# A row softmax on one core: sixteen-row transfers, and the scaling of 13 of 16 groups on GpSimd

## The chip, the core and the metric

The kernel runs on one core of a Trainium2 chip. Four of the core's engines matter: VectorE (DVE in the profile), ScalarE (ACT), GpSimd (POOL) and SyncE (SP, which only issues transfers here). Transfers between the memory of the chip (HBM) and the on-chip memory run on the core's 16 DMA engines; SP and ACT each feed a queue of them. The metric is device time in microseconds (us), the median of several runs.

## What is computed

A softmax over the last axis of 16 x 1024 x 512 numbers in fp32, that is 16384 rows of 512:

```python
x_max = np.max(x, axis=-1, keepdims=True)
exp_x = np.exp(x - x_max)
return (exp_x / np.sum(exp_x, axis=-1, keepdims=True)).astype(np.float32)
```

The input is 33.55 MB, the output as much. There is no matrix product.

## The kernel before

The 16384 rows are laid on 128 partitions, 128 rows of 512 to each. They are cut into eleven chunks. A chunk of R rows per partition is one load, for which each partition reads R consecutive rows. The chunks have 1, 3, 5, 7 and then seven times 16 rows (`CHUNKS`, line 13; the second number of each pair is the place in the on-chip tile). The tile `held` has room for 96 of the 128 rows of a partition (line 79), so the last two chunks go where the first ones and chunk 5 lay: load 9 is issued after the store of chunk 3 and load 10 after the store of chunk 4 (`AFTER_STORE`, line 20), and each waits until the stores that free its place have landed. The other nine loads are issued at the start (lines 138 and 139). Two of them, chunk 0 on ACT and chunk 1 on SP, are moved ahead of the barrier at which all engines meet at the start (`AT_HEAD`, line 30, and `loads_at_the_head`).

Work goes by groups of up to 8 rows per partition, 18 in all (lines 83 to 91). For each group:

- `rowmax` (line 102): DVE reduces the group to the negated maximum of each row, tile `shift`;
- `exps` (line 110): ACT takes the exponential of each row in place, one instruction a row, with `shift` as its bias, and the sum of the row as a by-product, tile `sums`. In the trace each is an ACTIVATE and an ACTIVATION_READ_ACCUMULATOR;
- `scale` (lines 122 and 124): DVE takes the reciprocals of the sums, tile `recip`, and multiplies each row by its own, one instruction a row;
- the store (line 130), issued on ACT's queue. It stands in ACT's order of instructions, behind whatever exponentials were emitted before it. Chunks 4, 5 and 6 are stored in halves of 8 rows (`STORE_ROWS`, line 26), the others whole.

The order is written out by hand (lines 137 to 150) and each engine keeps to it: maximum and exponentials of group g, then the scaling of group g - 1. At the four first changes of chunk (`FINISH_BEFORE`, line 24) the scaling of the earlier group comes before the maximum of the new one. Waits between engines, and between transfers and engines, are put in by the framework from what each instruction reads and writes.

GpSimd has nothing to do but four small MEMSETs at the start.

Of the kernel before, what the change touches and what calls it, by code (L numbers as in the profile page):

```python
# [1 line left out]

# [4 lines left out]

F32 = mybir.dt.float32
EXP = mybir.ActivationFunctionType.Exp
AX = mybir.AxisListType.X  # L10


CHUNKS = [
    (1, 0), (3, 1), (5, 4), (7, 9), (16, 16), (16, 32), (16, 48), (16, 64), (16, 80),
    (16, 0), (16, 16),
]
SBUF_ROWS = 96

EARLY = 9
AFTER_STORE = {3: [9], 4: [10]}  # L20

GROUP = 8

FINISH_BEFORE = (1, 2, 3, 4)

STORE_ROWS = {4: 8, 5: 8, 6: 8}

ON_ACT = (0,)

AT_HEAD = {mybir.EngineType.Activation: 1, mybir.EngineType.SP: 1}  # L30

def loads_at_the_head(nc):

    main, body = nc.main_func.blocks[0], nc.main_func.blocks[1]
    for engine, count in AT_HEAD.items():
        loads = [
            i
            for i in body.instructions  # L40
            if i.engine == engine and type(i).__name__ == "InstDMACopy"
        ][:count]
        barrier = next(
            n
            for n, i in enumerate(main.instructions)
            if i.engine == engine and type(i).__name__ == "InstDrain"
        )
        for load in loads:
            body.instructions.remove(load)
        main.instructions[barrier:barrier] = loads  # L50


@with_exitstack
def kernel(
    ctx: ExitStack,
    tc: tile.TileContext,
    x: bass.AP,
    out: bass.AP,
):
    nc = tc.nc  # L60
    nc.at_finalize(loads_at_the_head)
    P = nc.NUM_PARTITIONS

    x_flat = x.flatten_outer_dims()
    out_flat = out.flatten_outer_dims()
    n, d = x_flat.shape
    assert n == P * sum(R for R, _ in CHUNKS)


    src, dst, at = [], [], 0  # L70
    for R, _ in CHUNKS:
        for flat, views in ((x_flat, src), (out_flat, dst)):
            part = flat[at : at + P * R, :]
            views.append(part.rearrange("(p r) d -> p r d", r=R))
        at += P * R

    data = ctx.enter_context(tc.tile_pool(name="data", bufs=1))
    stats = ctx.enter_context(tc.tile_pool(name="stats", bufs=4))
    held = data.tile([P, SBUF_ROWS, d], F32, name="held")
    place = [held[:, s : s + R, :] for R, s in CHUNKS]  # L80


    groups = []
    for k, (R, _) in enumerate(CHUNKS):
        m = max(1, round(R / GROUP))
        cuts = [R * i // m for i in range(m + 1)]
        since = 0
        for a, b in zip(cuts, cuts[1:]):
            ends = b == R or b - since >= STORE_ROWS.get(k, R)
            groups.append((k, a, b, since if ends else None))  # L90
            since = b if ends else since
    shift = [None] * len(groups)
    sums = [None] * len(groups)

    def load(k):
        queue = nc.scalar if k in ON_ACT else nc.sync
        queue.dma_start(out=place[k], in_=src[k])

    def rowmax(g):
        k, a, b, _ = groups[g]  # L100
        shift[g] = stats.tile([P, b - a], F32, name="shift", tag="shift")
        nc.vector.reduce_max(  # L102
            out=shift[g], in_=place[k][:, a:b, :], axis=AX, negate=True
        )

    def exps(g):
        k, a, b, _ = groups[g]
        sums[g] = stats.tile([P, b - a], F32, name="sums", tag="sums")
        for r in range(a, b):
            nc.scalar.activation(  # L110
                out=place[k][:, r, :],
                in_=place[k][:, r, :],
                func=EXP,
                bias=shift[g][:, r - a : r - a + 1],
                scale=1.0,
                accum_out=sums[g][:, r - a : r - a + 1],
            )

    def scale(g):
        k, a, b, since = groups[g]  # L120
        recip = stats.tile([P, b - a], F32, name="recip", tag="recip")
        nc.vector.reciprocal(out=recip, in_=sums[g])  # L122
        for r in range(a, b):
            nc.vector.tensor_scalar_mul(  # L124
                out=place[k][:, r, :],
                in0=place[k][:, r, :],
                scalar1=recip[:, r - a : r - a + 1],
            )
        if since is not None:
            nc.scalar.dma_start(  # L130
                out=dst[k][:, since:b, :], in_=place[k][:, since:b, :]
            )
        if b == CHUNKS[k][0]:
            for later in AFTER_STORE.get(k, ()):
                load(later)

    with tc.manual_schedule():
        for k in range(EARLY):
            load(k)
        waiting = None  # L140
        for g, (k, a, _, _) in enumerate(groups):
            if waiting is not None and a == 0 and k in FINISH_BEFORE:
                scale(waiting)
                waiting = None
            rowmax(g)
            exps(g)
            if waiting is not None:
                scale(waiting)
            waiting = g
        scale(waiting)  # L150


# [1 line left out]
_INS = ['x']  # L154
_OUTS = [((16, 1024, 512), 'float32')]


# [23 lines left out]
```

## Time and profile before

| | us |
|---|---|
| median of 3 runs | 161.63 (161.62 to 161.69) |
| profiled execution, first to last instruction (span) | 160.1 |
| DVE busy | 124.2 |
| ACT busy | 93.4 |
| POOL busy | 0.2 |
| first maximum starts | 4.9 |
| last store issued | 146.4 |

The span is that of one execution under the profiler; the runs are timed from outside and hold 1.5 us more. The busy times are sums over an engine's instructions; issuing a transfer is not in them. In the lines below a group of instructions is given as: line, engine, operation, tile written <- tiles read, shapes (partitions x elements), count | total busy us, mean ns of one | idle time of the engine before them and what ended it. A line of DMA issues has the count, the size of each and the median time from issue to landing, which holds the time in the queue. The rows of digits divide the span into 40 slices of 4.0 us, with the busy share in tenths.

### The profile page before, as it was taken

How to read it: one execution, taken by the hardware profiler on the slowest of the kernel's cores; microseconds unless marked ns; L12 is line 12 of the kernel's file. 1: busy time of each engine (PE TensorE's matmuls, PEld its weight loads, DVE VectorE, ACT ScalarE, POOL GpSimd, SP SyncE). 2: the span in 40 equal slices, each digit the busy share in tenths (PEclk: the TensorE clock that was granted, in tenths of full speed). 3: DMA queues.
4: the chain of work that ended last, by engine and by line, in shares of the span. 5: the costliest groups of instructions: out<-in, count | busy, mean ns of one | idle time of the engine just before them, and what ended most of it. 6: DMA issues, size and time to landing. Idle time of an engine off the chain costs nothing.

```text
span 160.1 us, 525 instructions
## 1 busy us (share of the span) xinstructions
DVE 124.2 (78%) x164; ACT 93.4 (58%) x257; POOL 0.2 (0%) x4
## 2 busy tenths in 40 slices
DVE  0349094299699999999999999999999999935000
ACT  0550805604994959595959595959586867760000
POOL 0000000000000000000000000000000000000000
DMA  7999979989899999998999999999999999999993
GB/s 237 411 400 475 490 320 465 459 359 489 377 435 465 401 471 442 418 426 385 446 479 430 397 456 401 458 393 446 413 458 483 409 409 442 450 409 418 483 409 156
DMA packets 3603, 67.14 MB, mean 419 GB/s; under 512 B 400, under 2 KB 400, under 8 KB 912
## 3 DMA queue, kind: packets, MB, share of 16 engines
q10 hardware_dynamic: 2160, 33.82, 49.3%
q1 hardware_dynamic: 1440, 33.29, 49.1%
q14 instruction: 3, 0.02, 0.0%
HBM read 33.55 MB, written 33.55 MB: 419 GB/s over the span
## 4 chain that ended last, share of the span: by engine, by line
DVE 71%; ACT 15%; DMA 3%; issue 2%; DVEq 0%; ACTq 0%
DVE shift L102 39%; DVE held L124 30%; ACT held L110 14%; DMA held<-in_x_dram 3%; DVE recip L122 2%; ACT L110 1%; DVEq L176 0%; ACTq L110 0%
## 5 line engine op out<-in xcount | busy, mean ns | idle before, releaser
L110 ACT ACTIVATE held<-held,shift 128x512 f32<-128x512 f32 x128 | 90.5, 708 | 44.5 <-DVE shift L102 32.3
L102 DVE TENSOR_REDUCE shift<-held 128x8 f32<-128x4096 f32 (+4 forms) x18 | 70.8, 3938 | 4.9 <-DMA held<-in_x_dram 4.9
L124 DVE TENSOR_SCALAR held<-held,recip 128x512 f32<-128x512 f32 x128 | 52.3, 481 | 0.6
L110 ACT ACTIVATION_READ_ACCUMULATOR held<-held,shift 128x1 f32 x128 | 23.8, 186 | 0.0
L122 DVE RECIPROCAL recip<-sums 128x8 f32<-128x8 f32 (+4 forms) x18 | 3.4, 191 | 16.6 <-ACT held L110 16.6
L110 ACT ACT_TABLE_LOAD x1 | 1.3, 1283 | 4.9 <-DMA held<-in_x_dram 4.9
L165 POOL MEMSET const-bfloat16-1.0<- 128x1 bf16 x1 | 0.1, 102 | 0.0
L165 POOL MEMSET const-uint8-127<- 128x1 uint8 x1 | 0.1, 102 | 0.0
L165 POOL MEMSET const-float32-1.0<- 128x1 f32 x1 | 0.1, 99 | 0.0
L165 POOL MEMSET const-float32-0.0<- 128x1 f32 x1 | 0.1, 98 | 0.2 <-issue 0.2
## 6 DMA issues: line engine op xcount, KB each, us to landing
held<-in_x_dram SPq DMA_DIRECT2D x7, 4096.0 KB, 32.0
out_dram<-held ACTq DMA_DIRECT2D x4, 4096.0 KB, 19.8
out_dram<-held ACTq DMA_DIRECT2D x6, 2048.0 KB, 35.9
held<-in_x_dram SPq DMA_DIRECT2D x1, 1792.0 KB, 12.1
out_dram<-held ACTq DMA_DIRECT2D x1, 1792.0 KB, 27.0
held<-in_x_dram SPq DMA_DIRECT2D x1, 1280.0 KB, 8.0
out_dram<-held ACTq DMA_DIRECT2D x1, 1280.0 KB, 24.2
held<-in_x_dram SPq DMA_DIRECT2D x1, 768.0 KB, 4.6
```

The costliest lines, as they stand in the source:

```text
L102: nc.vector.reduce_max(out=shift[g], in_=place[k][:, a:b, :], axis=AX, negate=True)
L110: nc.scalar.activation(out=place[k][:, r, :], in_=place[k][:, r, :], func=EXP, bias=shift[g][:, r - a : r - a + 1], scale=1.0, accum_out=s ...
L122: nc.vector.reciprocal(out=recip, in_=sums[g])
L124: nc.vector.tensor_scalar_mul(out=place[k][:, r, :], in0=place[k][:, r, :], scalar1=recip[:, r - a : r - a + 1],)
L165: nc = _bacc.Bacc("TRN2", target_bir_lowering=False, num_devices=1)
```

## The change

All eight chunks now have 16 rows, and every load and store is one whole chunk of 4096 KB. The tile still has six places of 16 rows; six loads are issued at the start, load 6 after store 0 and load 7 after store 1. Only SP's first load stands ahead of the barrier. There are 16 groups of 8 rows, numbered from 0. For groups 0 to 12 the multiplication by the reciprocals is one GpSimd instruction over the whole group, with the 8 reciprocals of a partition broadcast along the rows; groups 13, 14 and 15 are scaled on DVE, row by row, as before. The reciprocals stay on DVE. Stores stay on ACT's queue. For chunks 0 to 3 a store is emitted one group later than it could be (`STORE_BEHIND`). The rule of `FINISH_BEFORE` goes, and the pool of the small tiles has 6 buffers for each of them in place of 4.

```diff
-CHUNKS = [
-    (1, 0), (3, 1), (5, 4), (7, 9), (16, 16), (16, 32), (16, 48), (16, 64), (16, 80),
-    (16, 0), (16, 16),
-]
-SBUF_ROWS = 96
-EARLY = 9
-AFTER_STORE = {3: [9], 4: [10]}
+CHUNK = 16
+CHUNKS = 8
+PLACES = 6
 GROUP = 8
-FINISH_BEFORE = (1, 2, 3, 4)
-STORE_ROWS = {4: 8, 5: 8, 6: 8}
-ON_ACT = (0,)
-AT_HEAD = {mybir.EngineType.Activation: 1, mybir.EngineType.SP: 1}
+STORE_BEHIND = [1, 1, 1, 1, 0, 0, 0, 0]
+LOAD_AFTER = {0: 6, 1: 7}
+ON_POOL = 13
+AT_HEAD = {mybir.EngineType.SP: 1}
...
+    def load(k):
+        nc.sync.dma_start(out=place(k), in_=x_rows[k])
+
+    def store(k):
+        nc.scalar.dma_start(out=out_rows[k], in_=place(k))
+        if k in LOAD_AFTER:
+            load(LOAD_AFTER[k])
...
     def scale(g):
-        k, a, b, since = groups[g]
-        recip = stats.tile([P, b - a], F32, name="recip", tag="recip")
+        recip = stats.tile([P, GROUP], F32, name="recip", tag="recip")
         nc.vector.reciprocal(out=recip, in_=sums[g])
-        for r in range(a, b):
+        if g < ON_POOL:
+            nc.gpsimd.tensor_mul(
+                out=rows(g),
+                in0=rows(g),
+                in1=recip.unsqueeze(2).to_broadcast([P, GROUP, d]),
+            )
+            return
+        for r in range(GROUP):
             nc.vector.tensor_scalar_mul(
...
     with tc.manual_schedule():
-        for k in range(EARLY):
+        for k in range(PLACES):
             load(k)
-        waiting = None
-        for g, (k, a, _, _) in enumerate(groups):
-            if waiting is not None and a == 0 and k in FINISH_BEFORE:
-                scale(waiting)
-                waiting = None
+        stored = 0
+        for g in range(groups):
             rowmax(g)
             exps(g)
-            if waiting is not None:
-                scale(waiting)
-            waiting = g
-        scale(waiting)
+            if g:
+                scale(g - 1)
+            if stored < CHUNKS and g > (stored + 1) * per - 1 + STORE_BEHIND[stored]:
+                store(stored)
+                stored += 1
+        scale(groups - 1)
+        while stored < CHUNKS:
+            store(stored)
+            stored += 1
```

`per` is 2, the groups of a chunk. So in ACT's order store 0 stands behind exponentials 3, stores 1, 2 and 3 behind exponentials 5, 7 and 9, store 4 behind exponentials 10, store 5 behind 12, store 6 behind 14 and store 7 at the end.

## The prediction

> **What bounds the kernel now.** I read the page's shares first, then the slices of DMA, the DMA issues, the chain, and last the windows of ten microseconds.
>
> ```profile
> span 160.1 us, 525 instructions
> DVE 124.2 (78%) x164; ACT 93.4 (58%) x257; POOL 0.2 (0%) x4
> DMA  7999979989899999998999999999999999999993
> HBM read 33.55 MB, written 33.55 MB: 419 GB/s over the span
> DVE 71%; ACT 15%; DMA 3%; issue 2%; DVEq 0%; ACTq 0%
> out_dram<-held ACTq DMA_DIRECT2D x6, 2048.0 KB, 35.9
> ```
>
> The reader is to see two full resources. The chain names DVE with 71%, but the chain follows instructions, and the last of them is the issue of a store. The DMA row stands at 9 or just under from the second slice to the last but one, and the 2 MB stores take 35.9 us from issue to landing: they stand in a queue. The windows say the same of both:
>
> ```profile
> 60.00:70.00 10.00, 9.96 (x17) 8.03 (x23) 0.00 (x0) 1.00 0.99 426
> 70.00:80.00 10.00, 9.96 (x14) 8.01 (x23) 0.00 (x0) 1.00 0.98 421
> 80.00:90.00 10.00, 9.96 (x11) 6.75 (x20) 0.00 (x0) 1.00 1.00 429
> ```
>
> Columns: window, its length, busy DVE, ACT and POOL, clock, DMA share, GB/s. The ten windows from 40 to 140 us have a mean of 432 GB/s. 33.55 + 33.55 = 67.1 MB at 432 GB/s is 155.4 us, so of the span of 160.1 only 4.7 us are not full-rate transfer, most of it in the first slice (237 GB/s over 4.0 us, 1.8 us lost) and the last (156 GB/s, 2.6 us lost). So the kernel is bound by **DMA**, with DVE full beside it from 34 to 143 us. Relief for DVE alone buys nothing. The most that better transfers can buy is a part of 4.7 us.
>
> The measured median is 161.63 us, 1.5 us over the profiled span of 160.1 (the part outside the first and last instruction); I add 1.5 to every span.
>
> **The change, part by part.** The rows that price it:
>
> ```profile
> L110 ACT ACTIVATE held<-held,shift 128x512 f32<-128x512 f32 x128 | 90.5, 708 | 44.5 <-DVE shift L102 32.3 <-issue 12.1
> L102 DVE TENSOR_REDUCE shift<-held 128x8 f32<-128x4096 f32 x14 | 61.7, 4411 | 0.0
> L124 DVE TENSOR_SCALAR held<-held,recip 128x512 f32<-128x512 f32 x128 | 52.3, 481 | 0.6
> L165 POOL MEMSET const-float32-1.0<- 128x1 f32 x1 | 0.1, 99 | 0.0
> ```
>
> and from the chain in order of time (start, length, what), the steps of one group of 8 rows, out of the last two groups:
>
> ```profile
> 132.66 4.34 DVE shift L102
> ...
> 137.08 5.76 ACT held L110 x16
> 142.83 0.02 issue
> 142.86 0.21 DVE recip L122
> 143.07 0.03 issue
> 143.10 0.49 DVE held L124
> ```
>
> So a group costs 4.4 us for the maximum (DVE), 5.8 for the exponentials with their sums (ACT), 0.3 for the reciprocal with its handovers and 3.3 for the scaling (the chain shows the eight multiplications of a full group as one piece of 3.26 us).
>
> *Removed from DVE:* 13 groups x 3.26 = 42.4 us of scaling. By the first part it buys nothing by itself, as DMA is the bound.
>
> *Added on POOL:* 13 instructions of 128x4096, each with two operands, the tile and the broadcast reciprocals. No row shows POOL do arithmetic, so I call its time P and bound it. From below: the reduction reads the same 128x4096 once in 4.41 us, and P should not be less than one such pass. From above: a pass for each operand and one for the result, 3 x 4.41 + 0.10 (POOL's own MEMSET of one element) = 13.3 us. I take 2 x 4.41 + 0.10 = **8.92 us**: the row nearest to it is the reduction, whose time goes by the elements it reads, and this instruction has twice as many operand elements. 13 x 8.92 = 116.0 us. Both ends stay for the range.
>
> The Trainium skill bears on this row ("GPSIMD Engine Reference", section 3.1): it gives a two-input elementwise operation on GpSimd 4497 ns at 2048 fp32 elements against 2293 on VectorE, and advises VectorE for such work. That speaks against the change; doubled it would be an estimate of 8.99 us, and the sum below would be 0.9 us longer.
>
> *Who waits for POOL.* The groups of POOL follow one another: a group's exponentials cost ACT 5.8 us against 8.92, so POOL is never short of work after its first. A store is issued by ACT, in order with the exponentials, and waits there for both its POOL groups. Behind store k stand the exponentials of the next groups, so ACT falls into POOL's pace: the store of chunk 5 stands ahead of exponentials 13 (groups counted from 0) and waits for POOL group 11. The sum from the start:
>
> - First load, now 16 rows, 4.19 MB: lands at 11.5 us. At 432 GB/s it is 9.7 us; in the trace of before the first three slices (237, 411, 400 GB/s) have moved that much by 12.0 us in small pieces. I take 11.5; the ends move the sum by -1.8 and +0.5.
> - Maximum 0, exponentials 0, reciprocal 0: 4.4 + 5.8 + 0.3, so POOL starts at 22.0.
> - 13 groups on POOL: 22.0 + 116.0 = 138.0.
> - DVE scales group 13. Its reciprocal is there at 22.0 + 12P + 5.8 + 0.4, which is P - 6.2 = 2.7 us before POOL ends group 12. Whether it may run beside POOL the trace can't show; the wait costs 0 to 2.7 us. I take 2.7: DVE's scaling passes 512 elements in 3.26 / 8 = 0.41 us, the reduction in 4.33 / 8 = 0.54, so it draws on the memory harder than the reductions that run beside POOL. Scaling 13 ends at 141.3.
> - Behind it on DVE stands maximum 15 (it was put after scaling 13 by the loop): 145.7. Exponentials 15: 151.5. Reciprocal and scaling 15: 155.1.
> - Last store, 4.19 MB with nothing before it in the queue (store 6 was issued at 141.3 and is through by 153): 9.7 us plus the start and landing. The last store of before took 12.9 us from issue to landing, with some backlog in it; I take 11.6, landed at 166.7. The ends are -1.9 and +1.3.
> - The span of before ends 0.85 us after its last landing: 167.6. With 1.5: **169.1 us**.
>
> In short T = 53.1 + 13P, and 160 to 162 needs P between 8.2 and 8.4.
>
> The rule on this wait in the Trainium skill ("SBUF — State Buffer", "Who interferes with whom") is that a VectorE operation in a 2-port mode, `tensor_scalar` among them, and a GpSimd instruction lock each other out for a whole instruction, while reductions don't contend. By it the sum keeps the 2.7 us; without it 166.4. The trace of before, in which POOL does nothing, shows neither.
>
> *Transfers of 16 rows.* Bytes stay the same. The small loads and stores at the start go, which gives DMA larger pieces from the first: by the slices 1 to 1.5 us of the 4.7 can come back, and would show only if DMA stayed the bound. Six loads follow each other at once, 58 us of work for DMA, so the four waits of SP for earlier loads (21.2 us in all) go, and nothing was idle in them. What the larger first load costs is the first compute, at 11.5 us instead of 4.9; before, DVE and ACT could start on one row. On the path through POOL these 6.6 us count in full (they are in the sum).
>
> *One load ahead of the barrier, not two:* ACT's load of one row goes. Nothing: the load on SP keeps DMA at work for 9.7 us, and the second SP load of before left within 1 us.
>
> *Early stores a group later:* store 0 waits for POOL group 1, at 22.0 + 17.8 = 39.8 us, about when exponentials 3 end (22.0 - 0.3 + 3 x 5.8 = 39.1). So it costs ACT nothing at first, while the loads fill DMA to 58 us; without that cover it would be an idle DMA. Loads 6 and 7 wait for the landing of stores 0 and 1, near 60 and 80 us. The eight loads and stores 0 to 3 (store 3 is issued at 22.0 + 8P = 93.4) are 12 transfers of 9.7 us; DMA fed from 1 us on has done them, load 7 among the last, at about 117. Maximum 14 wants load 7 after exponentials 12, at 22.0 + 10P + 12 = 123: a cover of 6 us. After 117 the queue is empty: stores 4 to 7 come at POOL's pace, one in 17.8 us for 9.7 us of transfer. There the idle time of DMA opens.
>
> **The rivals.**
>
> *DMA stays the bound* (the other side). If P is under about 8.2 us, the queue never runs dry, and only the start gets better: 160.1 - 1.5 + 1.5 = **160.0 us**, faster. For it: the bound from below is 4.41, and DVE, which is full now, gets 42 us of air. Against it: two operands in one instruction. The point that decides is P = 8.2.
>
> *DVE's scaling runs beside POOL:* 169.1 - 2.7 = **166.4 us**.
>
> *POOL is slower than two passes:* at P = 9.5 it is 176.6, at the upper bound 13.3 it is 226. The MEMSET of 99 ns shows a cheap start of an instruction and speaks against a large fixed cost, but not against a slow loop.
>
> *The change doesn't do what it says:* the stores "a group later" are not later by a group but by POOL's queue, as computed; this is in the sum and no case of its own.
>
> **How the numbers follow.** Forecast, P of 8.4 to 9.5 and DVE waiting: 0.50, at 169.1. DVE beside POOL: 0.12, at 166.4. DMA the bound: 0.28, at 160.0. POOL over 9.5: 0.10. The first case's own range is 162 to 176.5. The range of all starts under the DMA case, 158.8, and ends at 176.5; the 0.10 above it is left out, though the upper bound of P would reach there. Within 0.2% (161.3 to 162.0, about what a measurement can tell from no change) lies P near 8.4: 0.03, taken from the first two cases. Faster 0.28, slower 0.69.
>
> **What would show it.** In the changed profile: POOL TENSOR_TENSOR x13 with a mean of 8.9 us and POOL busy some 116 us in an unbroken row; ACT waiting for POOL at its stores; DMA slices at 9 to about 117 us and gaps after; the first multiplication of group 13 starting as POOL ends; the last store landing in under 12.9 us. DMA full to the end and POOL's mean under 8.2 would make the prediction wrong, as would POOL pauses between groups, which would mean ACT is the slower one.

## The result and the profile after

The changed kernel takes **162.92 us** (median of 4 runs, 162.19 to 164.09) against 161.63: the ratio is 1.0083, with a 95% interval of 1.0055 to 1.0111. Measured twice more, beside the kernel before on other chips, its ratio was 1.0061 (1.0031 to 1.0092) and 1.0022 (1.0002 to 1.0043). It is slower, as forecast, but by 0.2 to 0.8%, not by 4.6%: the prediction missed the size. Runs more than 1.5% above the fastest of their kernel, taken as a slow state, are left out of the medians, ratios and counts below (two of twelve of b0 and of b1, and five of ten of a2, whose profiled execution is one of them and serves for places only), so long runs may be commoner than the counts say.

The page of the changed kernel, the lines that answer to those shown of before:

```profile
span 160.4 us, 425 instructions
...
DVE 82.0 (51%) x56; ACT 92.7 (58%) x257; POOL 91.0 (57%) x17
...
DMA  7999999999899999999999999999999999999993
...
HBM read 33.55 MB, written 33.55 MB: 418 GB/s over the span
...
DMA 53%; POOL 14%; DVE 10%; ACT 7%; issue 7%; DVEq 0%; SPq 0%
...
L107 POOL TENSOR_TENSOR held<-held,recip 128x4096 f32<-128x4096 f32 x13 | 90.8, 7018 | 31.5 <-DVE recip L105 31.5
L89 DVE TENSOR_REDUCE shift<-held 128x8 f32<-128x4096 f32 x16 | 70.2, 4393 | 46.9 <-DMA held<-in_x_dram 46.9
```

DVE went from 124.2 to 82.0 us busy, 42.2 us less against a forecast of 42.4, and it bought nothing, as forecast. The surprise stands in the POOL line: one group takes 7.02 us, not 8.92. POOL stood idle for 31.5 us in all, after its start too, and DVE waited 46.9 us for loads (12.3 of them for the first). DMA is full from the second slice to the last but one. So what was lost should show inside the DMA row. This execution took 162.19 us, the fastest of the four, and its span is only 0.3 us longer than that of before: it can show where the transfers gain and lose, but not the whole 1.3 us between the medians. The windows, of before and then of after (columns: window, its length, busy DVE, ACT, POOL, clock, DMA share, GB/s):

```profile
0.00:12.00 12.00, 3.23 (x6) 4.32 (x9) 0.20 (x4) 1.00 0.91 350
12.00:35.00 23.00, 14.12 (x20) 8.67 (x24) 0.00 (x0) 1.00 1.01 428
35.00:47.00 12.00, 10.43 (x10) 8.65 (x25) 0.00 (x0) 1.00 1.00 432
47.00:120.00 73.00, 72.69 (x93) 54.50 (x152) 0.00 (x0) 1.00 1.01 433
120.00:157.00 37.00, 23.74 (x39) 17.25 (x48) 0.00 (x0) 1.00 1.01 437
```

```profile
0.00:12.00 12.00, 0.00 (x0) 0.00 (x0) 0.20 (x4) 1.00 0.96 393
12.00:35.00 23.00, 18.89 (x8) 19.56 (x53) 12.20 (x2) 1.00 1.00 432
35.00:47.00 12.00, 9.67 (x5) 12.00 (x35) 12.00 (x3) 1.00 1.00 390
47.00:120.00 73.00, 34.50 (x16) 47.71 (x135) 63.89 (x10) 1.00 1.00 431
120.00:157.00 37.00, 18.95 (x29) 13.45 (x38) 2.71 (x1) 1.00 1.01 437
```

By these rows the start gained (393 - 350) x 12 / 432 = 1.2 us, as the larger first pieces promised, and from 35 to 47 us the kernel gave it back: (432 - 390) x 12 / 432 = 1.2 us. The rows are coarse, though. Each counts a piece where it starts, and sixteen pieces of 32 KB are 44 GB/s in 12 us, so a row can even show more than the 432 GB/s at which sixteen engines move such pieces in 1.21 us each. With each piece of the packet records spread over its own time, the gain is 0.5 us up to 12 us (365 GB/s against 346) and 0.5 us from 12 to 35 (433 against 424), and the loss from 35 to 47 is 1.1 us (394 against 432). Rates marked "spread" below are worked out in this way; the sum is the same, a gain of about 1 us and a loss of about 1 us.

Store 0 is issued at 36.8. In the packet records the pieces of 32 KB of the loads in flight, which take 1.21 us before and after, take 1.5 to 2.5 us between 38 and 42 us, and each of the 16 DMA engines loses about 1 us of reading. The first piece of store 0 itself is on record at 40.7 us, so most of the slow reads come ahead of it. I call this **the stop**, though the pieces slow down and do not halt.

### The profile page after: what moved, and what is told of

It reads as the page before. It is cut to its first block, busy times and chain, and to the rows that moved or that the text cites. A ratio compares the mean times of both kernels' runs of the same rounds, so it can differ in the third digit from the quotient of the medians.

```text
span 160.4 us, 425 instructions
## 1 busy us (share of the span) xinstructions
DVE 82.0 (51%) x56; ACT 92.7 (58%) x257; POOL 91.0 (57%) x17
## 4 chain that ended last, share of the span: by engine, by line
DMA 53%; POOL 14%; DVE 10%; ACT 7%; issue 7%; DVEq 0%; SPq 0%
DMA held<-in_x_dram 34%; DMA out_dram<-held 19%; POOL held L107 14%; ACT held L94 7%; DVE shift L89 6%; DVE held L114 4%; DVE recip L105 0%; DVEq L161 0%; SPq L72 0%; DVEq L105 0%; DVEq L89 0%
## 5 line engine op out<-in xcount | busy, mean ns | idle before, releaser
L107 POOL TENSOR_TENSOR held<-held,recip 128x4096 f32<-128x4096 f32 x13 | 90.8, 7018 | 31.5 <-DVE recip L105 31.5
L89 DVE TENSOR_REDUCE shift<-held 128x8 f32<-128x4096 f32 x16 | 70.2, 4393 | 46.9 <-DMA held<-in_x_dram 46.9
L94 ACT ACTIVATION_READ_ACCUMULATOR held<-held,shift 128x1 f32 x128 | 25.3, 198 | 0.0
L105 DVE RECIPROCAL recip<-sums 128x8 f32<-128x8 f32 x16 | 3.2, 200 | 16.0 <-ACT held L94 16.0
L114 DVE TENSOR_SCALAR held<-held,recip 128x512 f32<-128x512 f32 x24 | 9.8, 483 | 0.1
L94 ACT ACT_TABLE_LOAD x1 | 1.3, 1283 | 12.3 <-DMA held<-in_x_dram 12.3
```

Source lines behind the costliest of these rows:

```text
L89: nc.vector.reduce_max(out=shift[g], in_=rows(g), axis=AX, negate=True)
L94: nc.scalar.activation(out=rows(g)[:, r, :], in_=rows(g)[:, r, :], func=EXP, bias=shift[g][:, r : r + 1], scale=1.0, accum_out=sums[g][:, ...
L107: nc.gpsimd.tensor_mul(out=rows(g), in0=rows(g), in1=recip.unsqueeze(2).to_broadcast([P, GROUP, d]),)
L114: nc.vector.tensor_scalar_mul(out=rows(g)[:, r, :], in0=rows(g)[:, r, :], scalar1=recip[:, r : r + 1],)
```

## The experiments

Theory A: the loss is the stop, and belongs to the transfers. Theory B: it is GpSimd's work. Later theories stand in the expectations, beginning with C, one DMA engine that falls behind the other fifteen. The kernels of one letter ran on one chip, with the kernel before beside them at 161.63 to 161.72 us.

**a1, no GpSimd:** the transfers alone.

```diff
-ON_POOL = 13
+ON_POOL = 0
```

> The changed kernel with all 16 groups scaled on DVE, as in the kernel before; the transfers stay at 16 rows. Theory A (the loss sits in the transfers: reads slow down for a moment when the first 4 MB store meets a full queue of loads, at 39 to 42 us in the profile of the changed kernel, 1 us lost): the span stays at 160.4 to 162.3 us over the runs, and only the part outside the span goes from 1.8 to 1.5 us; median 162.4 to 162.9. Theory B (GpSimd's work costs the time, by a disturbance of the transfers or of ACT): the span falls to 159.5 to 160.1 and the median to 161.0 to 161.6, with runs as close together as those of the kernel before. DVE has 16 x (4.4 + 0.3 + 3.3) = 128 us of work from 12.3 us on, which ends near 146 with the last exponentials between: no later than in the changed kernel (last store issued at 145.0), so DVE should not become the bound under either theory.

Measured 161.86, ratio 1.0011 (0.9997 to 1.0025), twelve runs of 161.45 to 162.50. Neither theory: the stop is there (393 GB/s from 35 to 47 us, store 0 at 39.6), and yet the kernel is level with before. The part outside the span is 1.8 us here, in the changed kernel and in before alike.

**a2, stores later:**

```diff
-STORE_BEHIND = [1, 1, 1, 1, 0, 0, 0, 0]
+STORE_BEHIND = [3, 3, 2, 2, 1, 1, 0, 0]
```

> The changed kernel with stores 0 and 1 emitted three groups later than they could be, 2 and 3 two groups, 4 and 5 one (in the changed kernel 1, 1, 1, 1, 0, 0). Store 0 then stands behind exponentials 5 and leaves near 51 us, not 36.8. Theory A: the slow reads move with store 0, from 39 to 42 us to 52 to 57 us, and the loss stays; median 162.5 to 163.5. Theory B: nothing moves, the slow stretch stays near 40 us or is absent; median 162.9 as it was. Under both, if loads 6 and 7, which wait for stores 0 and 1, come too late, DMA shows idle slices after 60 us and the time grows by their length.

Ratio 1.0058 (1.0034 to 1.0083). Store 0 left at 46.4, and the stop moved with it:

```profile
35.00:47.00 12.00, 9.70 (x5) 12.00 (x36) 12.00 (x3) 1.00 1.01 437
47.00:59.00 12.00, 9.65 (x5) 12.00 (x37) 12.00 (x3) 1.00 0.99 396
```

The window in which the changed kernel had 390 GB/s has 437, and the next one, which had 434, has 396. The stop goes where store 0 goes.

**a3, the kernel before with GpSimd scaling its first 15 groups:**

```diff
+        on_pool = g < 15
+        if on_pool:
+            nc.gpsimd.tensor_mul(
+                out=place[k][:, a:b, :],
+                in0=place[k][:, a:b, :],
+                in1=recip.unsqueeze(2).to_broadcast([P, b - a, d]),
+            )
-        for r in range(a, b):
+        for r in range(b if on_pool else a, b):
```

(and 6 buffers for the small tiles)

> The kernel before with its chunks and transfers, but the first 15 of its 18 groups (104 of 128 rows) scaled on GpSimd, one instruction a group; the last three on DVE; small tiles with 6 buffers. Theory A: the transfers are those of before, so the span stays near 160.1 to 160.5 and the median is 161.6 to 162.1, the difference being the part outside the span. Theory B: GpSimd's work costs its 1 us here too, median 162.6 or more. GpSimd's time by the changed kernel's 7.02 us for 8 rows: 104 / 8 x 7.02 = 91 us, which is no bound.

Measured 161.49, ratio 0.9990 (0.9982 to 0.9999), eleven runs of 161.34 to 161.72. GpSimd worked for 91 us and cost nothing. Theory B falls for these transfers; whether GpSimd's work costs something beside loads and stores of 16 rows is another question, which a3 does not ask. No stop shows with the small first stores (430 GB/s from 35 to 47 us, spread).

**a4, every other group:** the odd groups up to 11 on GpSimd, groups 5 and 9 in halves.

```diff
-        if g < ON_POOL:
-            nc.gpsimd.tensor_mul(out=rows(g), ...)
+        if g % 2 == 1 and g < ON_POOL:
+            step = 4 if g in (5, 9) else GROUP
+            for r in range(0, GROUP, step):
+                nc.gpsimd.tensor_mul(
+                    out=rows(g)[:, r : r + step, :], ...
```

> The changed kernel with only the odd groups up to 11 on GpSimd, the others on DVE; groups 5 and 9 in two halves of 4 rows (128x2048). It prices one GpSimd instruction: if the time goes by elements alone, a half takes 3.51 us; with a fixed cost f a half is 3.51 + f/2. And it shows whether DVE's multiplications wait for a running GpSimd instruction, as the prediction assumed: then groups of eight on DVE that fall beside GpSimd take up to 7 us longer than 3.26, or start late with their reciprocal long done. Theory A: median 162.3 to 163; theory B, with half of GpSimd's work: 162.0 to 162.5.

Measured 161.42, ratio 0.9993 (0.9982 to 1.0004). Its groups of instructions by shape:

```profile
L116 DVE TENSOR_SCALAR held<-held,recip 128x512 f32<-128x512 f32 x80 | 38.5, 552 | 0.4
L109 POOL TENSOR_TENSOR held<-held,recip 128x4096 f32<-128x4096 f32 x4 | 28.1, 7017 | 55.9 <-DVE recip L105 55.9
L109 POOL TENSOR_TENSOR held<-held,recip 128x2048 f32<-128x2048 f32 x4 | 14.3, 3602 | 15.1 <-DVE recip L105 15.1
```

Two halves less a whole are 2 x 3.602 - 7.017 = 0.19 us of fixed cost; the rest is 1.67 ns an element. Other sizes lie on the same line: 1.04 us for 512 elements and 6.16 for 3584 in a3, 1.90 for 1024 in c3. And the answers for DVE's multiplications and for one overlap in the timeline:

```profile
L116 DVE TENSOR_SCALAR held<-held,recip x80: 471/475/1579, 22.8 to 142.4; 128x512 f32<-128x512 f32 x80
```

```profile
30.52 7.02 POOL L109 TENSOR_TENSOR held<-held,recip 128x4096 f32<-128x4096 f32 x1 [30.09 <-DVE recip L105]
...
36.15 0.20 DVE L105 RECIPROCAL recip<-sums 128x8 f32<-128x8 f32 x1 [1.42 <-ACT held L94]
...
36.39 4.21 DVE L116 TENSOR_SCALAR held<-held,recip 128x512 f32<-128x512 f32 x8
```

Eight multiplications took 4.21 us instead of 3.26. The first started at 36.39 and ended at 37.82, 0.28 us after POOL's instruction, which ended at 37.54; the other seven took 0.475 us each. The same happened all six times that DVE started to scale beside POOL: the first multiplication took 1.43 to 1.58 us and ended 0.28 us after POOL. DVE's scaling does wait for a running GpSimd instruction, as the prediction chose. In the same stretch the reductions kept their 4.4 us.

**b0, the changed kernel again:**

> The changed kernel once more, beside the kernel before on one chip, for its spread: so far 4 runs of 162.2 to 164.1, while the kernel with half of GpSimd's groups had ten runs of 161.3 to 162.2 and the one with none twelve of 161.5 to 162.5. Theory C (one of the 16 DMA engines falls behind the others and the last store waits for it; this happens with 16-row transfers and GpSimd at work without a pause): median 162.5 to 163.2, runs 1 to 3 us apart, and the last landings show one engine 1 to 3 us behind the other fifteen. Rival D (the four runs were chance): median 161.4 to 162.0 and runs within 1 us.

Ratio 1.0061. Seven of the ten runs lie at 161.75 to 162.34, three at 163.65 to 163.98: two heaps, with nothing between on this chip (the other two measurements have runs of 162.66, 162.75 and 163.18). The profile taken is of the first heap (span 160.3), so what makes the second isn't shown here; b1 and e2 have a trace of such a run.

**b1, seven groups on GpSimd:**

```diff
-ON_POOL = 13
+ON_POOL = 7
```

> The changed kernel with groups 0 to 6 on GpSimd and 7 to 15 on DVE. GpSimd then works without a pause to about 72 us and not at all after. Theory C in its first form (GpSimd at work makes an engine fall behind): about half of the loss stays, median 162.0 to 162.5. Rival E (the loss comes from the start: the moment of store 0 and the stretch after it, which is the same as in the changed kernel up to 72 us): the whole loss stays, 162.5 to 163.2. Rival D: 161.4 to 161.9.

Ratio 1.0046 (1.0020 to 1.0073), runs of 161.56 to 163.75, two of the ten over 163.6. The profiled run is one of these (163.75): fifteen of the sixteen landings of its last store come between 157.8 and 159.4 us, one at 161.1. So one engine is late, as theory C has it, and GpSimd, which ended at 71.5, isn't needed after that: theory E is nearer than the first form of C.

**b2, halves of stores:**

```diff
-        nc.scalar.dma_start(out=out_rows[k], in_=place(k))
+        for h in range(0, CHUNK, GROUP):
+            nc.scalar.dma_start(
+                out=out_rows[k][:, h : h + GROUP, :], in_=place(k)[:, h : h + GROUP, :]
+            )
```

> The changed kernel with each store cut in two of 8 rows per partition, both issued where the whole one was; loads stay at 16 rows. Bytes and order stay. A load then gets two thirds of a DMA engine beside a store, where it had a half (289 against 143 GB/s in the kernel before). If the size of a store's pieces makes the reads stop at store 0 or an engine fall behind, both get smaller: median 161.3 to 161.9. If not: as the changed kernel beside it.

161.98, ratio 1.0026 (1.0013 to 1.0039), twelve runs, none over 162.62. No run lies in the second heap, and the stop is somewhat smaller (407 GB/s from 35 to 47 us; spread 405, against 399 for b0): a part.

**b3, a small first store:** one row per partition of chunk 0 ahead of the other 15.

```diff
+            if g == 1:
+                nc.scalar.dma_start(
+                    out=out_rows[0][:, :1, :], in_=place(0)[:, :1, :]
+                )
```

> The changed kernel with one row per partition (256 KB) of chunk 0 stored by itself as soon as group 0 is scaled, near 30 us, and the other 15 rows where store 0 was. If the slow reads after store 0 are the price of the first store of any size, they move to 30 to 35 us and are gone at 39 to 42; if they come with a large store against a full queue of loads, they stay at 39 to 42 us and nothing shows at 31. If they are spread over the pieces, the loss of about 1 us shrinks to some 0.3, as it was with the small first stores of the kernel before. Time: 0 to 0.8 us below the changed kernel beside it.

162.42, ratio 1.0046 (1.0031 to 1.0061). Nothing shows at 31 us (442 GB/s from 23 to 35); the reads slow when the 15 rows go out (393 from 35 to 47). So it is not the price of the first store of any size.

**c1, loads 1 to 5 on ACT's queue:**

```diff
-        nc.sync.dma_start(out=place(k), in_=x_rows[k])
+        queue = nc.scalar if 1 <= k <= 5 else nc.sync
+        queue.dma_start(out=place(k), in_=x_rows[k])
```

> The changed kernel with loads 1 to 5 issued on ACT's queue ahead of its first work, and load 0, 6 and 7 on SP's. The stores then stand in one queue behind the loads: store 0 starts when load 5 is through, near 60 us, and two queues share the engines only while loads 6 and 7 run. Bytes and the order of the work stay. Theory A, second form (the reads stop for a moment when a store's queue joins a running queue of loads): nothing slow at 38 to 42 us; something of the kind may show near 70 us, when load 6 joins the stores. Median 0.5 to 1 us below the changed kernel's lower runs (162.0), so 161.0 to 161.5. Rival F (the reads stop whenever the first large store goes out, whatever the queues): the slow stretch sits near 60 us and the median stays at 162 or above.

161.84, ratio 1.0013 (0.9999 to 1.0026), eleven runs, none over 162.54. From 35 to 47 us there were 432 GB/s; the slow pieces, some 0.7 us per engine, stand at 57 to 60 us, where the queue passes from load 5 to store 0. Rival F is right on the place (it had put the time at 162 or above), and the second form of theory A falls: the stop takes no second queue.

**c2, the same queues with a4's groups:** both edits above (no halves).

> The same queues, with only the odd groups up to 11 on GpSimd. With half of GpSimd's groups and two queues it was 161.42 us with one stop of 0.65 us at 38 to 42 us. Theory A, second form: 160.8 to 161.2 us, below both kernels. Rival F: 161.4 as it was.

161.68, ratio 1.0004 (0.9990 to 1.0018); the stop was again at 57 to 60 us. Nothing gained on a4.

**c3, GpSimd made as slow as predicted:** a second instruction in each of its groups, on two rows, by a tile of ones.

```diff
+            nc.gpsimd.tensor_mul(
+                out=rows(g)[:, 0:2, :],
+                in0=rows(g)[:, 0:2, :],
+                in1=ones.unsqueeze(2).to_broadcast([P, 2, d]),
+            )
```

> The changed kernel with a second GpSimd instruction in each of the 13 groups that multiplies two of its rows by ones (128x1024). By the two sizes measured (3.60 us for 128x2048, 7.02 for 128x4096, so 0.19 + 1.67 ns an element) it takes 1.9 us, and a group costs GpSimd 8.9 us, which is what the prediction took P to be. The prediction's sum with that P, 53.1 + 13 x 8.9, gives 168.8 us; without DVE's wait for GpSimd's last group 166.1. If the chain of the prediction was right but for P, the time is 167.5 to 170, GpSimd works without a pause from 22.8 to about 138.5 us, and DMA has idle slices after 117 us. If DMA still hides it, the time is 162 to 163 and the sum was wrong beyond P.

**169.34 us**, ratio 1.0474 (1.0455 to 1.0493). Its page and two windows:

```profile
GB/s 274 477 383 493 376 485 391 464 415 430 336 469 399 469 399 454 423 438 438 407 469 383 477 399 479 383 485 391 462 415 258 376 376 250 446 424 133 376 376 250
...
L115 POOL TENSOR_TENSOR held<-held,ones 128x1024 f32<-128x1024 f32 x13 | 24.7, 1898 | 1.0
```

```profile
140.00:150.00 10.00, 9.55 (x15) 5.78 (x17) 0.00 (x0) 1.00 0.74 315
150.00:160.00 10.00, 3.46 (x9) 1.97 (x6) 0.00 (x0) 1.00 0.61 262
```

POOL's groups follow one another from 22.8 to 139.2 us, 8.95 us each; from slice 31 on the transfers come in bursts with gaps (258, 250, 133 GB/s). With P = 8.95 the prediction's sum is 53.1 + 116.4 = 169.5. The end of the chain, from the timeline:

```profile
136.70 5.16 DVE L122 TENSOR_SCALAR held<-held,recip 128x512 f32<-128x512 f32 x8
...
137.25 1.95 POOL L115 TENSOR_TENSOR held<-held,ones 128x1024 f32<-128x1024 f32 x1
...
141.78 4.41 DVE L92 TENSOR_REDUCE shift<-held 128x8 f32<-128x4096 f32 x1
...
155.60 0.34 ACTq L78 DMA_DIRECT2D out_dram<-held  x1
```

The last store lands at 166.7, and the span ends at 167.5.

**c4, one-operand instructions:** groups 2 to 5 scaled on GpSimd row by row.

```diff
+        if 2 <= g < 6:
+            for r in range(GROUP):
+                nc.gpsimd.tensor_scalar_mul(
+                    out=rows(g)[:, r, :], in0=rows(g)[:, r, :], scalar1=recip[:, r : r + 1],
+                )
+            return
```

> The changed kernel with groups 2 to 5 scaled on GpSimd row by row, one operand tile of 128x512 and a number per partition, 8 instructions a group. It asks whether GpSimd's time goes by operand elements: 7.02 us is 0.19 + 8192 operand elements x 0.83 ns. Then a row costs 0.19 + 512 x 0.83 = 0.62 us and a group 4.9 us. If the time goes by results and not by operands, a row costs 0.19 + 512 x 1.67 = 1.05 us and a group 8.4. The time of the kernel should stay where it is, 162 to 163, in the first case.

```profile
L108 POOL TENSOR_SCALAR held<-held,recip 128x512 f32<-128x512 f32 x32 | 49.3, 1568 | 0.0
L115 POOL TENSOR_TENSOR held<-held,recip 128x4096 f32<-128x4096 f32 x9 | 62.9, 7022 | 22.3 <-DVE recip L105 22.3
```

Both expectations missed: a row takes 1.57 us, three ns an element and so more, not less, with one operand. GpSimd's time does not go by operand elements across kinds of instruction. The 32 rows lie within 1.562 and 1.573 us. The one run took 165.58 us, not the 162 to 163 expected. POOL's work adds up to 49.3 + 62.9 = 112.2 us, and the prediction's sum with that in place of 13P gives 165.3.

**d1, d2, d3, d4:** can the stop be avoided, and the late engine? d1 (a4's groups) and d3 (the changed kernel's) store chunk 0 in growing pieces and chunk 1 in halves; d2 is a4's groups with b2's halves; d4 is a3 with chunks of 4 and 12 ahead of the sixteens and the odd groups on GpSimd.

```diff
+FIRST = (0, 1, 4, 8)
+            if g == 1:
+                for lo, hi in zip(FIRST, FIRST[1:]):
+                    nc.scalar.dma_start(
+                        out=out_rows[0][:, lo:hi, :], in_=place(0)[:, lo:hi, :]
+                    )
...
-    (1, 0), (3, 1), (5, 4), (7, 9), (16, 16), ...
+    (4, 0), (12, 4), (16, 16), ...
```

> The changed kernel with the odd groups up to 11 on GpSimd and the others on DVE, and chunk 0 stored in pieces of 1, 3, 4 rows per partition as soon as group 0 is scaled (near 26 us), then 8; chunk 1 in two halves; the rest whole. Without the pieces it was 161.42 us, with a stop of the reads worth 0.65 us at 38 to 42 us. If a store that is large against what went before is what stops the reads, the stop is gone or under 0.2 us and the median is 160.7 to 161.1, below both kernels. If the stop belongs to the end of a long stretch of pure reads, it sits at 26 to 32 us and the median stays 161.3 to 161.6.

163.10, ratio 1.0096 (1.0072 to 1.0119). The stop at store 0 is gone (spread, 432 GB/s from 23 to 35 us and 428 from 35 to 47), and the time is longer: the transfers slow elsewhere, 412 GB/s from 59 to 71 us and 407 from 95 to 107 (spread, 424 and 418).

> The same share of GpSimd (odd groups up to 11), all stores in two halves of 8 rows per partition, each pair issued where the whole store was. Halves on the changed kernel gave 161.98 us against 162.2 and no run over 162.7; half of GpSimd's groups gave 161.42. If the two act on the same thing, 161.3 to 161.6; if they add up, 161.0 to 161.2.

163.24, ratio 1.0094 (1.0081 to 1.0107), with 412 GB/s both from 35 to 47 us and from 95 to 107 (spread, 416 and 404). The guess that halves help by themselves falls.

> The changed kernel with all 13 groups on GpSimd and chunk 0 stored in pieces of 1, 3, 4 rows after group 0 (near 30 us), then 8; chunk 1 in halves. If the late engine comes from the stop at store 0, and the stop from the size of the first store: no run over 162.7, median 161.0 to 161.6. If it comes from GpSimd working without a pause: a part of the runs over 163.5, as in the changed kernel.

163.79, ratio 1.0134 (1.0109 to 1.0158); nothing at store 0 (427 from 35 to 47), then 393 GB/s from 95 to 107 us (spread, 431 and 399).

> The kernel before with chunks of 4, 12 and seven times 16 rows instead of 1, 3, 5, 7 and seven times 16, its stores in pieces of 4, 6, 6 and 8 rows up to the last four chunks, and the odd groups up to 13 on GpSimd. The first store leaves near 15 us. With the small chunks and most groups on GpSimd the kernel before had 161.49 us, no stop of the reads, and slow small pieces in the first 10 us (404 to 430 GB/s against 433). If stores that start early avoid the stop and larger first pieces win back a part of the start, 160.8 to 161.3. If the stop returns with the larger first load, 161.4 to 161.8.

162.13, ratio 1.0024 (1.0010 to 1.0038). No gain either: its first store leaves at 20.9 us, two more at 34 to 37, and from 35 to 47 us there are 408 GB/s (spread, 418), a stop of 0.4 us. These four ran without the changed kernel beside them, so what this chip makes of it isn't known.

**e1 and e2, a4 and the changed kernel side by side:**

> The kernel with the odd groups up to 11 on GpSimd (groups 5 and 9 in halves) once more. If its 161.42 us is its own and not that chip's: 161.3 to 161.8, at least 0.4 below the changed kernel beside it. If chips differ in how they serve 16-row transfers: it moves with the changed kernel, 162 to 163.

> The changed kernel a third time, beside the one above. From its 16 runs so far: median 162.0 to 162.9, a part of the runs over 163.5, with one DMA engine late.

e1 took 161.45, ratio **0.9983** (0.9973 to 0.9993), e2 161.81, ratio 1.0022. On one chip, then, half of GpSimd's groups are 0.4% faster than all 13. With that a4's kernel and a3 are the fastest that were found, by 0.1 to 0.2%, and can't be told apart; over its two chips a4's 19 runs lie between 161.16 and 162.16. e2's profiled execution is one from the second heap (163.63 us, span 161.8), e1's is 161.45. The last microseconds of e1 and of e2:

```profile
156.00:158.00 2.00, 0.00 (x0) 0.00 (x0) 0.00 (x0) 1.00 0.69 295
158.00:160.00 2.00, 0.00 (x0) 0.00 (x0) 0.00 (x0) 1.00 0.00 0
```

```profile
156.00:158.00 2.00, 0.00 (x0) 0.00 (x0) 0.00 (x0) 1.00 0.69 295
158.00:160.00 2.00, 0.00 (x0) 0.00 (x0) 0.00 (x0) 1.00 0.23 98
```

Both have the stop (393 GB/s from 35 to 47 us), and both have 295 GB/s from 156 to 158. Then e1 is through, and e2 still moves 98 GB/s, less than a quarter of the rate: a few engines are late. The landing records say the same; each transfer has sixteen, one for each engine, though without the engine's name. Those of the last store of e1 lie between 157.8 and 158.8 us; in e2 the first is at 157.8 and the last three are at 161.0. Stores 4, 5 and 6 of e2 look alike: the last three landings are 3.1 to 3.2 us after the first (store 4: 128.8 to 132.0, in e1 128.8 to 129.9). So three engines are late by store 4 and do not catch up. At store 0 nothing sets e2 apart yet (59.8 to 62.7, in e1 60.0 to 63.0); where the lateness begins isn't shown.

## Why the prediction was right or wrong, point by point

**The bound of the kernel before, and DVE's relief:** right. DMA was the bound, and some 42 us less of DVE (82.7 us busy in a3) gave next to nothing: a ratio of 0.9990.

**The step that failed is the time of one GpSimd instruction.** It was put as "2 x 4.41 + 0.10 = 8.92 us" and came to 7.02, so that the term of 116.0 us is 91.2. The bounds held (4.41 and 13.3), and the fixed cost was near (0.19, estimated at 0.10); the choice between the bounds was not. It took DVE's pace per element read, 1.08 ns, and set it on another engine, twice for each result; GpSimd's two-operand product needs 1.67 ns a result. With P at 7.02 the sum by POOL is 144.3 us, less than the transfers need, and so the chain through POOL never became the bound. A crossover at 8.2 with a value taken at 8.92, from ends of 4.41 and 13.3, was no ground for an even chance of a 4.6% loss.

The Trainium skill's figure ("GPSIMD Engine Reference", section 3.1: 4497 ns at 2048 fp32 elements) would have missed by a little more: 3602 ns were measured at that size, for a product with a broadcast operand where the page times an addition. The measurement decides. Its advice that such work is cheaper on VectorE holds by the same rows, 3.26 us against 7.02.

**The chain through GpSimd:** right, and shown. c3, with P at 8.95, took 169.34 where the sum gives 169.5; c4, with another mixture, took 165.58 where it gives 165.3. Behind POOL in c3, maximum 15 and exponentials 15 had their sizes; the end of scaling 13 came 2.7 us after POOL's (3.3 in the sum) and the last store took 11.1 us (11.6). Against that POOL started at 22.8, not 22.0, and the part outside the span was 1.8, not 1.5. So the agreement within 0.2 us is in part errors that cancel, and luck to that extent.

**DVE's wait for GpSimd:** right as a mechanism (a4); in c3 it cost 1.9 us (5.16 less 3.26) and not 2.7, since one multiplication passed between the two GpSimd instructions of the last group. In the changed kernel it costs nothing, since POOL's last group ends at 122.7 us and DVE's first scaling starts at 128.0. The rule on the shared port in the Trainium skill ("SBUF — State Buffer", "Who interferes with whom") agrees with a4: multiplications blocked to the end of GpSimd's instruction (1.43 to 1.58 us for the first), reductions not (4.4 us).

**The rival "DMA stays the bound"** was the true case, for the reason given (P under 8.2), with the wrong time: 160.0 against 161.8 to 162.9. Three terms of it were off.

- The part outside the span is 1.8 us in the runs of both kernels, not 1.5. The profiled execution of before was a little longer than the median, and the subtraction mixed the two. 0.3 us.
- The gain of 1 to 1.5 us at the start came (1.0 us, spread) and went again in the stop at store 0 (1.1 us). The prediction gave "all stores a group later" no price beyond idle DMA, and no row of before showed a 4 MB store against a long run of loads. a2 and c1 show that the stop goes where store 0 goes, a3, d1 and d3 that first stores that start small and grow have none.
- In a part of the runs one or a few engines end 2 to 3 us late, as e2's trace shows for one of them: 6 of the 26 runs of the changed kernel lie between 163.1 and 164.1.

**Loads 6 and 7:** "a cover of 6 us" was wrong in its direction. Load 7 landed at 123.4, not 117, and with the faster POOL maximum 14 wanted it long before; DVE waited 8.8 us. Load 6 had landed at 104.0 in the same way, and from this came the pause of 6.1 us of POOL before 108.7; it did not mean a slow ACT, as the prediction's sign of being wrong had it. It cost nothing that the windows show, because the queue was never empty (431 GB/s from 47 to 120 us).

**What stays open.** Why the reads stop at the first large store isn't shown; size matters (b2, b3), the second queue doesn't (c1). Why engines fall late isn't either. It was seen with GpSimd at work without a pause up to 72 us and stores of 16 rows in a second queue (the changed kernel, b1), and not in a1, a4, b2 or c1, each of which changes one of these. But their profiles are of one run each, a1 and a4 ran on a chip on which the changed kernel was not run, and d1 and d2, on yet another chip, were slow without the first condition, by slow transfers at 95 to 107 us. That GpSimd and the large transfers cost time only together, which a1, a3 and a4 would allow, is not settled: on one chip, halving GpSimd's work brought 0.4% in e1 against e2, and no clear difference in b1 against b0. And with the stop at store 0 gone in d1 and d3 the time did not fall, so the stop can't be said to cost the time that its own window shows, nor to cost nothing, as the changed kernel was not run on that chip. Chips may differ, too: the changed kernel's ratio was 1.0083, 1.0061 and 1.0022 in its three measurements.

## What to carry to other kernels

A price that the profile doesn't have should be measured before a forecast hangs on it: one run of a single GpSimd instruction in two sizes would have given 7.02 us, which is under the 8.2 on which this forecast turned. When the transfers are the bound, look at the DMA row in windows, since a gain at the start can be given back where the traffic changes from loads to stores, and at the last engine to land, since it and not the mean sets the end. GpSimd can take elementwise work from a busy VectorE at 1.67 ns an element as long as something else is the bound, in one large instruction with a broadcast operand and not row by row with a number per partition (7.02 us a group against 12.5).

## What the runs showed of the hardware

- GpSimd's product with a broadcast operand takes 0.19 us + 1.67 ns an element; its product with one number per partition takes 1.57 us for 512 elements, 3.1 ns each with whatever of it is fixed (c4, one size only).
- DVE's row-by-row scaling waits for a running GpSimd instruction to end: its first multiplication took 1.43 to 1.58 us instead of 0.475 and ended 0.28 us after it, six times in a4, while a reduction beside it kept its 4.4 us.
- The first large store against a run of loads slows the pieces of the loads in flight from 1.21 us to as much as 2.5, once, and costs 0.7 to 1.1 us on each engine (a4, c1 and the changed kernel).
- ACT issued store 0 of the changed kernel at 36.8 us, the moment POOL was done, though three exponentials that stand ahead of it in ACT's order started only after that, at 37.2, 37.9 and 38.6: here the issue of a transfer did not wait for the exponentials before it.
